# Value groups of the past, one at a time or in pairs, beside a dense prompt attention on one core

## The chip, the cores and the metric

The kernel runs on one core of one Trainium2 chip. The metric is device microseconds for one call, from the first to the last instruction on the core with what the runtime puts around it; lower is better. The engines are named as in the profile: PE (matmul), PEld (its weight loads), DVE (vector), ACT (scalar), POOL (GpSimd) and SP, which here computes nothing and only issues DMAs. Each engine executes its own instructions in the order in which they were written into its queue; what one engine needs from another is guarded by a semaphore.

## The reference, cut to what matters

One decoder layer is computed for 512 prompt tokens and for 8 sample tokens (one new token for each of 8 samples). Beside the prompt's own attention, each sample attends to 1024 past tokens that lie in 8 pages of 128 rows in a paged cache:

```python
v_all = jnp.concatenate([cache_v[page_table].reshape(DB, P, N_HEADS, HEAD_DIM), v], axis=1)
s = jnp.einsum("bqhd,bkhd->bhqk", q, k_all) * scale
s = s + Fk[:, :, P:, None] - Fk[:, :, None, :]
p = jax.nn.softmax(s, axis=-1)
return jnp.einsum("bhqk,bkhd->bqhd", p, v_all)
```

The last line, restricted to the past, is the part at issue: for 8 samples and 8 pages, a weighted sum over the 128 rows of a page of 1024 floats (512 KB), for each of 16 heads. Everything is float32; the dense products are made of three products of rounded halves (`hi`, `lo`) each.

## The kernel before, in words

Feature-major activations of 520 columns (512 prompt, 8 sample) stand in SBUF as 8 tiles of 128 partitions. The kernel runs one long list of products: `product()` takes one block of 128 weight columns, runs 24 matmuls over the first 260 columns, evacuates, and 24 over the second 260. `begin()`, at the head of each product, advances `state["n"]`, loads the weights ahead (`load_chunks`, on SP's queue) and splits them into halves ahead (`split_upto`: ACT writes `whi`, DVE writes `wlo`).

**The past's values.** The 8 samples go in four pairs `r`; pair `r` and page `j` make one *value group*, 32 groups in all (`values_todo`). `sample_values(r, j)` (L830 to L852) computes one group: four matmuls of 512 columns, each into its own 32 partitions of one PSUM bank `pv` through `tile_position=(0, 32 * gq)`, so that they use four strips of 32 columns of the array. A float32 matmul is two instructions in the trace, so that a group is eight PE instructions at L839. With the last page of a pair (`j == 7`) DVE masks and folds the bank into `dr`; two groups into the next pair (`j == 2`) `fold_values` runs one small matmul `pvs` (L854) and an ACT copy. `pw[r]`, the weights, comes from `past_softmax(r)`, a chain of steps of which `tick()` runs one at a time; `lgt` (L795) is one of its matmuls.

**The pages.** `page_load` reads a page's number into a register and issues one DMA of 512 KB into a tile of the pool `pgp` (7 buffers of 4 KB per partition, shared with pages of keys and, at other times, with other loads). Up to `state["n"] == 41` POOL issues it, later SP. `value_pages` loads one group ahead: its list `ahead` holds at most one group. The pool `heap` has 60 buffers ("slots") of 2080 bytes per partition, which `slot()` hands out for nearly all other tiles; an instruction that writes a tile waits until the last reader of the buffer's previous tile is through.

**When.** `tick(keys, values)` adds `values` to `state["due"]` and lets at most one group run. In the first 42 products it is called from `begin()`; ten groups run there. The attention then runs eight iterations `i`, one for each pair of heads. In iteration `i` the order on PE is: first half of the product `k` of `i+1`; **part 0** (`mid_a`: the transposes `vt` of `v_tokens`, then `at(i, 0)`); second half of `k`; the transposes `ptt` of `turn(i, 0)`; **part 1** (`at(i, 1)`); first half of the product `v`; `mid_b` with the transposes of `turn(i, 1)`, the scores of blocks 0 and 1 of `i+1` (L1245, L1246) and **part 2**; second half of `v`; `values(i)` (`po`, L1302); scores of blocks 2 and 3; **part 3** (`at(i, 3)`, not in the last iteration). In the last iteration the products are `gb`, and `turn(7, 0)` stands in part 0. The table `VALUES_AT` says how many groups fall due in each part: the remaining 22 groups run one by one in part 0 (8), part 1 (8) and part 3 (6). `in_place()` ties what a tick issues on PE, DVE and ACT behind the last product's matmul and the last split.

The steps that the prediction follows are the softmax of a pair of heads (DVE L1252, ACT L1253, reciprocal L1255, scaling by ACT or POOL at L1259), the casts of transposed probabilities (`ph` on ACT L1272, `pl` on DVE L1273) and the weight split (ACT L246, DVE L248).

Of the kernel before, what the change touches and what calls it, by code (L numbers as in the profile page):

```python
# [25 lines left out]
NPAGE = 8  # L26
# [39 lines left out]
def kernel(ctx, tc, xT, par, gates, b_f, cst, cse, own, cache_k, cache_v, cache_lf, pt,  # L66
# [13 lines left out]
    def slot(name, cols=NT, dt=F32, parts=128):  # L80
        return heap.tile([parts, cols], dt, name=name, tag="slot")

    def bank(name, parts=128, cols=512):
        return psp.tile([parts, cols], F32, name=name, tag="bank")
# [96 lines left out]
    state = {"n": 0, "dma": 0, "split": 0, "load": 22, "lead": 11, "due": 0, "age": 1}  # L181
# [8 lines left out]
    def flush():  # L190
        while stores:
            sp.dma_start(*stores.pop(0))
# [92 lines left out]
    def begin(last=None):  # L285
        n = state["n"]
        state["n"] += 1
        last = len(units) - 1 if last is None else last
        if n == 1:
            split_upto(reach(n, last, state["lead"]))  # L290
        if n < 42:
            tick(KEYS[n], n in VALUES)
        load_chunks(units[reach(n, last, state["load"])][0])
        split_upto(reach(n, last, state["lead"]))
        flush()
        return n
# [19 lines left out]
    @contextmanager  # L316
    def in_place():

        with tc.issue_after(state["mm"].ins), tc.issue_after(state["last"].ins), tc.issue_after(state["act"].ins):
            yield  # L320
# [371 lines left out]
    def page_load(cache, s, j, pg=None, c0=0, c1=D):  # L692
        if pg is None:
            pg = pgp.tile([128, D], F32, name="pg", tag="pg")
        n = s * NPAGE + j
        eng = pool if state["n"] <= LAST_POOL else sp
        done = loads[eng]
        with tc.issue_after(done[-4].ins) if len(done) >= 4 else nullcontext():
            r = eng.value_load(ptb[0:1, n:n + 1], min_val=0, max_val=NPOOL - 1)
        done.append(eng.dma_start(pg, cache[bass.ds(r, 1), :, c0:c1].rearrange("a p c -> (a p) c")))  # L700
        return pg
# [30 lines left out]
    def key_sums():  # L732
        for p in pend:
            p[0] += 1
        while pend and pend[0][0] >= (state["age"] if state["n"] < 43 else 1000):
            with tc.issue_after(state["qadd"].ins):
                key_sum()
# [19 lines left out]
    def key_pages(n):  # L757
        for _ in range(n):
            if keys_todo:
                key_page(*keys_todo.pop(0))  # L760
# [3 lines left out]
    chains = []  # L764
    pw = [None] * 4

    def tick(keys, values):
        state["age"] = 1 if state["n"] < 5 else 2
        key_sums()
        with in_place():  # L770
            for c in list(chains):
                c[0] += 1
                if c[0] >= 2:
                    c[0] = 0
                    if next(c[1], True):
                        chains.remove(c)
            state["due"] += values
            state["due"] -= some_values(min(1, state["due"]))
        value_pages()
        key_pages(keys)  # L780

# [50 lines left out]
    def sample_values(r, j):  # L832
        if j == 0:
            pv[0] = bank(f"pv{r}")
        pgs = ahead.pop(0)
        for gq in range(4):
            c = 32 * j + 8 * gq
            hf = gq % 2
            pe.matmul(pv[0][32 * gq:32 * gq + 32, :], lhsT=pw[r][:, c:c + 32],  # L839
                      rhs=pgs[gq // 2][:, 512 * hf:512 * hf + 512], start=j == 0, stop=j == NPAGE - 1,  # L840
                      tile_position=(0, 32 * gq))
        if j == NPAGE - 1:
            pw[r] = None
            dr = slot("dr", 512)
            dve.tensor_tensor(dr, pv[0], pvm, ALU.mult)
            for n in (256, 128):
                dve.tensor_tensor(dr[:, :n], dr[:, :n], dr[:, n:2 * n], ALU.add)
            pv["todo"] = r, dr
        elif j == 2 and "todo" in pv:
            fold_values(*pv.pop("todo"))  # L850

    def fold_values(r, dr):  # L852
        ps = bank(f"pvs{r}")
        pe.matmul(ps[:, :16], lhsT=dr[:, :128], rhs=cs[:, C_SEL:C_SEL + 16], start=True, stop=True)  # L854
        act.copy(pvt.rearrange("p (h c s) -> p c s h", h=2, c=4)[:, :, 2 * r:2 * r + 2],
                 ps[:, :16].rearrange("p (c s h) -> p c s h", c=4, s=2))

    values_todo = [(r, j) for r in range(4) for j in range(NPAGE)]
    ahead = []

    def value_pages():
        if values_todo and not ahead and (pw[values_todo[0][0]] is not None or chains):
            r, j = values_todo[0]
            ahead.append([page_load(cache_v, 2 * r + a, j) for a in range(2)])

    def some_values(n):
        done = 0
        while done < n and values_todo and pw[values_todo[0][0]] is not None:
            value_pages()
            sample_values(*values_todo.pop(0))  # L870
            value_pages()
            done += 1
        return done


# [500 lines left out]
    scores(0, (2, 3))  # L1376
    g = None
    state.update(load=14, lead=8)
    VALUES_AT = [(1, 1, 0, 1)] * 4 + [(1, 1, 0, 0)] + [(1, 1, 0, 1)] * 2 + [(1, 1, 0, 0)]
    KEYS_AT = [(0, 0, 2, 0)] * 3 + [(0, 0, 0, 0)] * 5  # L1380

    def at(i, part):
        tick(KEYS_AT[i][part], VALUES_AT[i][part])
        flush()

    for i in range(KT):
# [40 lines left out]
        if not last:  # L1427
            scores(i + 1, (2, 3))
            at(i, 3)
        else:  # L1430
            some_values(32)
            assert not values_todo and not chains
            fold_values(*pv.pop("todo"))
# [360 lines left out]
```

## Time and profile before

| | before |
|---|---|
| three timed runs | 1016.21, 1017.39 and 1019.45 us |
| median | 1017.39 us |
| span of the profiled execution | 1016.4 us, first to last instruction (its own time with what lies around the span is not listed apart from the three runs) |
| PE busy | 994.3 us, 98% of the span |
| DVE, ACT, POOL busy | 797.3, 547.5 and 327.6 us |
| attention, first to last value group in it | 355.23 us to 527.9 us of the span |

The page's shares of busy time are averages over the whole span; a PE row of the timeline shows start, duration, line, tile, shape and, in brackets, idle time before it and what ended that. The durations of matmul rows overlap, since matmuls are pipelined, so that the distance between two *starts* is what an instruction costs.

### The profile page before, as it was taken

The page shows a single profiled execution, that of the slowest core. Times are in us where ns is not written, and L with a number is a line of the kernel's source. Part 1 is how long each engine was busy: PE and PEld are TensorE (multiplying, and loading weights), DVE is VectorE, ACT ScalarE, POOL GpSimd, SP SyncE. Part 2 cuts the span into 40 slices and gives each one's busy share as a digit, 9 for nine tenths or more (in the row PEclk, how much of TensorE's full clock was granted, in tenths as well). Part 3 has the DMA queues.
Part 4 walks back from the last instruction along what each step waited for, and adds up shares of the span by engine and source line. Part 5 has one row for each costly group of instructions (what it writes and reads, how often), then busy time and mean ns, then how long its engine had stood idle before and what let it go on. Part 6 is the DMA issues. An engine that isn't in the chain of part 4 may idle for free.

```text
span 1016.4 us, 21281 instructions
## 1 busy us (share of the span) xinstructions
PE 994.3 (98%) x8012; PEld 921.1 (91%) x8012; DVE 797.3 (78%) x1423; ACT 547.5 (54%) x1128; POOL 327.6 (32%) x415
## 2 busy tenths in 40 slices
PE   5999999999999999999999999999999999999996
PEld 2799999999998988888888888999999999999996
DVE  5559999998999888886655544869988888888764
ACT  4534576848761576777783233554444444445553
POOL 0346111121143245653400001583442442425112
PEclk9999999999999999999999999999999999999998
DMA  9798857788879998995867995324234243233122
GB/s 325 250 324 279 242 189 202 243 261 278 281 250 345 331 312 286 321 294 190 251 216 269 319 340 186 84 74 115 81 108 125 63 125 98 70 104 105 63 64 85
DMA packets 164378, 206.97 MB, mean 204 GB/s; under 512 B 9827, under 2 KB 125043, under 8 KB 164211
## 3 DMA queue, kind: packets, MB, share of 16 engines
q1 hardware_dynamic: 147634, 152.78, 48.1%
q0 software_dynamic: 12960, 46.41, 13.8%
q10 hardware_dynamic: 3680, 6.42, 1.7%
q8 instruction: 63, 1.03, 0.4%
q14 instruction: 41, 0.33, 0.1%
HBM read 192.49 MB, written 13.09 MB: 202 GB/s over the span
## 4 chain that ended last, share of the span: by engine, by line
PE 93%; DMA 2%; DVE 2%; ACT 1%; issue 0%; SPq 0%; POOL 0%; DVEq 0%; POOLq 0%; ACTq 0%
PE fo L307 12%; PE k L307 5%; PE wo L307 5%; PE gb L307 5%; PE gr L307 5%; PE v L307 5%; PE ga L307 5%; PE xr L307 5%; PE pb L307 4%; PE pv L839 3%; PE pa L307 3%; PE po L1302 2%; PE qp L542 2%; PE q L542 2%; PE ada L374 2%; PE ptt L1268 2%
## 5 line engine op out<-in xcount | busy, mean ns | idle before, releaser
L246 ACT CAST whi<-wraw 128x1024 fp32r<-128x1024 f32 (+1 forms) x79 | 82.0, 1039 | 113.6 <-PE pb L307 34.3
L248 DVE TENSOR_TENSOR wlo<-wraw,whi 128x1024 fp32r<-128x1024 f32 (+1 forms) x79 | 99.1, 1256 | 19.0 <-ACT whi L246 16.6
L307 PE MATMUL fo<-ach,wb 128*128 128x260 f32 x512 | 93.4, 283 | 0.0
L270 ACT CAST wb<-ws 128x512 fp32r<-128x512 f32 x72 | 44.7, 621 | 86.0 <-PE fo L307 58.9
L700 POOL DMA_DIRECT2D pg<-in_cache_k_dram x74 | 39.6, 536 | 143.1 <-DVE S L751 62.6
L271 DVE TENSOR_TENSOR wb<-wraw,wb 128x512 fp32r<-128x512 f32 x86 | 76.4, 889 | 4.7 <-ACT wb L270 3.9
L307 PEld LDWEIGHTS fo<-ach,wb 128*128 128x128 f32 x512 | 78.9, 188 | 0.0
L271 DVE TENSOR_TENSOR wb<-ws,wb 128x512 fp32r<-128x512 f32 x72 | 68.7, 954 | 12.6 <-ACT wb L270 11.0
L261 POOL TENSOR_TENSOR ws<-wraw 128x512 f32<-128x512 f32 x18 | 24.4, 1353 | 153.2 <-DMA wraw<-in_w_fi_dram 104.1
L307 PE MATMUL fo<-acl,wb 128*128 128x260 f32 x256 | 72.2, 282 | 0.0
L270 ACT CAST wb<-wraw 128x512 fp32r<-128x512 f32 x86 | 53.5, 622 | 31.4 <-ACT cp L1683 6.2
L750 DVE TENSOR_TENSOR pg<-pg,qb 128x1024 f32<-128x1024 f32 x48 | 57.9, 1221 | 2.5 <-DMA pg<-in_cache_k_dram 2.5
L751 DVE TENSOR_REDUCE S<-pg 128x16 f32<-128x1024 f32 x48 | 57.4, 1209 | 0.2
L1259 POOL TENSOR_SCALAR p<-p,mu 128x128 f32<-128x128 f32 (+3 forms) x28 | 38.4, 1381 | 53.0 <-DVE mu L1255 47.1
L307 PEld LDWEIGHTS fo<-acl,wb 128*128 128x128 f32 x256 | 48.2, 188 | 0.0
L1253 ACT ACTIVATE p<-p,mu 128x128 f32<-128x128 f32 (+3 forms) x64 | 35.4, 554 | 18.2 <-DVE mu L1252 18.0
L307 PE MATMUL v<-hh,whi 128*128 128x260 f32 x128 | 38.2, 298 | 0.8 <-ACT row L819 0.5
L307 PE MATMUL k<-hh,whi 128*128 128x260 f32 x128 | 37.3, 292 | 0.0
L307 PE MATMUL pb<-oh,whi 128*128 128x260 f32 x128 | 37.1, 290 | 0.2 <-ACT oh L1360 0.2
L307 PE MATMUL gb<-hh,whi 128*128 128x260 f32 x128 | 37.0, 289 | 0.0
L307 PE MATMUL v<-hl,whi 128*128 128x260 f32 x128 | 36.9, 288 | 0.0
L307 PE MATMUL v<-hh,wlo 128*128 128x260 f32 x128 | 36.9, 288 | 0.0
(1101 smaller groups left out, 3957.3 us busy)
## 6 DMA issues: line engine op xcount, KB each, us to landing
araw<-in_ada_w_dram SPq DMA_DIRECT2D x48, 512.0 KB, 7.6
wraw<-in_w_fi_dram SPq DMA_DIRECT2D x44, 512.0 KB, 5.3
pg<-in_cache_k_dram POOLq DMA_DIRECT2D x42, 512.0 KB, 6.2
pg<-in_cache_v_dram SPq DMA_DIRECT2D x42, 512.0 KB, 5.5
wraw<-in_w_in_dram SPq DMA_DIRECT2D x34, 512.0 KB, 6.4
wraw<-in_w_in_dram SPq DMA_DIRECT2D x11, 1024.0 KB, 8.5
pg<-in_cache_v_dram POOLq DMA_DIRECT2D x22, 512.0 KB, 6.1
pg<-in_cache_k_dram POOLq DMA_DIRECT2D x32, 256.0 KB, 5.9
```

Of the source, the lines that this page charges most:

```text
L246: state["act"] = act.copy(hi[:, :k1 - k0], src)
L248: state["last"] = dve.tensor_tensor(lo[:, :k1 - k0], src, hi[:, :k1 - k0].bitcast(F32), ALU.subtract)
L270: state["act"] = act.copy(t[:, :4], src)
L271: state["last"] = dve.tensor_tensor(t[:, 4:], src, t[:, :4].bitcast(F32), ALU.subtract)
L307: state["mm"] = pe.matmul(out[:, :t1 - t0], lhsT=wt[k], rhs=at, start=k == 0 and m == 0, stop=k == nk - 1 and m == 2)
L542: state["mm"] = pe.matmul(b[:, :HALF], lhsT=wt, rhs=at[:, t0:t1], start=k == 0 and m == 0, stop=k == 3 and m == 2)
L700: done.append(eng.dma_start(pg, cache[bass.ds(r, 1), :, c0:c1].rearrange("a p c -> (a p) c")))
L750: dve.tensor_tensor(pg, pg, q, ALU.mult)
L751: last = dve.tensor_reduce(S[r // 2][:, c:c + H], pg.rearrange("p (h d) -> p h d", d=DH), AX.X, ALU.add)
L839: pe.matmul(pv[0][32 * gq:32 * gq + 32, :], lhsT=pw[r][:, c:c + 32], rhs=pgs[gq // 2][:, 512 * hf:512 * hf + 512], start=j == 0, stop=j == ...
L1253: act.activation(p[:, :n + 128], p[:, :n + 128], AF.Exp, bias=mu[:, 0:1], scale=-1.0, accum_out=mu[:, 1:2])
L1259: (pool.tensor_scalar(p, p, mu[:, 2:3], None, ALU.mult) if a and i + 1 < KT else act.activation(p, p, AF.Copy, scale=mu[:, 2:3]))
```

## The change

The ticks of the attention run two value groups back to back where they ran one: `depth()` is 2 from the 43rd product on, `tick` lets up to `depth()` groups run, and `VALUES_AT` makes the groups due in twos, in part 1 of every iteration and in part 3 of iterations 0, 2 and 4. Two groups are then loaded ahead. The first group's pages still go to `pgp`; each page of the second group is loaded in two halves of 512 columns into two slots of `heap`, by two DMAs of 256 KB. The matmuls themselves, their operands' shapes and their number stay.

```diff
             state["due"] += values
-            state["due"] -= some_values(min(1, state["due"]))
+            state["due"] -= some_values(min(depth(), state["due"]))
...
-                      rhs=pgs[gq // 2][:, 512 * hf:512 * hf + 512], start=j == 0, stop=j == NPAGE - 1,
+                      rhs=pgs[gq // 2][hf], start=j == 0, stop=j == NPAGE - 1,
...
+    def depth():
+        return 2 if state["n"] >= 43 else 1
+
+    def value_page(s, j, halves):
+        if halves:
+            return [page_load(cache_v, s, j, slot("pgv", 512), 512 * a, 512 * a + 512) for a in range(2)]
+        pg = page_load(cache_v, s, j)
+        return pg[:, :512], pg[:, 512:]
+
     def value_pages():
-        if values_todo and not ahead and (pw[values_todo[0][0]] is not None or chains):
-            r, j = values_todo[0]
-            ahead.append([page_load(cache_v, 2 * r + a, j) for a in range(2)])
+        while values_todo[len(ahead):] and len(ahead) < depth():
+            r, j = values_todo[len(ahead)]
+            if pw[r] is None and not chains:
+                break
+            ahead.append([value_page(2 * r + a, j, len(ahead) == 1) for a in range(2)])
 
     def some_values(n):
         done = 0
+        value_pages()
         while done < n and values_todo and pw[values_todo[0][0]] is not None:
-            value_pages()
+            if not ahead:
+                value_pages()
             sample_values(*values_todo.pop(0))
-            value_pages()
             done += 1
+        value_pages()
         return done
...
-    VALUES_AT = [(1, 1, 0, 1)] * 4 + [(1, 1, 0, 0)] + [(1, 1, 0, 1)] * 2 + [(1, 1, 0, 0)]
+    VALUES_AT = [(0, 2, 0, 2), (0, 2, 0, 0), (0, 2, 0, 2), (0, 2, 0, 0), (0, 2, 0, 2)] + [(0, 2, 0, 0)] * 3
```

## The prediction, made before the changed kernel was run

> **What bounds the kernel now.** I read the page first: the busy shares, then the chain of work that ended last.
>
> ```profile
> span 1016.4 us, 21281 instructions
> PE 994.3 (98%) x8012; PEld 921.1 (91%) x8012; DVE 797.3 (78%) x1423; ACT 547.5 (54%) x1128; POOL 327.6 (32%) x415
> PE 93%; DMA 2%; DVE 2%; ACT 1%; issue 0%; SPq 0%; POOL 0%; DVEq 0%; POOLq 0%; ACTq 0%
> ```
>
> PE works through 98% of the span and carries 93% of the chain. What the change takes from PE's queue is time, and what it makes PE wait for is time; nothing else counts directly. Next the tile `pv`:
>
> ```profile
> L839 PE MATMUL pv<-pg,pw x256: 589/593/617, 195.7 to 527.3; 128*32 128x512 f32 x128
> ```
>
> 256 instructions are 32 groups of eight; 22 of the groups lie in the attention. The 593 ns mislead, since four strips run beside each other. What a group costs is seen between the starts around it, in PE's timeline. Here are the end of the scores and the start of `k`, with a group between them and without one:
>
> ```profile
> 396.95 0.39 PE L1246 MATMUL sc<-ksB,qlB 128*128 128x512 f32 x1
> 397.27 1.06 PE L839 MATMUL pv<-pg,pw 128*32 128x512 f32 x8
> 398.27 0.39 PE L307 MATMUL k<-hh,whi 128*128 128x260 f32 x1
> 398.50 0.28 PE L307 MATMUL k<-hh,wlo 128*128 128x260 f32 x1
> ...
> 469.84 0.39 PE L1246 MATMUL sc<-ksB,qlB 128*128 128x512 f32 x1
> 470.07 0.28 PE L307 MATMUL k<-hh,whi 128*128 128x260 f32 x1
> 470.19 0.28 PE L307 MATMUL k<-hh,wlo 128*128 128x260 f32 x1
> ```
>
> From the last score to the second matmul of `k` it is 1.55 us with a group and 0.35 us without: **one group costs 1.20 us**. It starts late (0.32 us after a score, where `k` follows after 0.23), and the first `k` matmul behind it takes 0.23 us instead of 0.12.
>
> **The change part by part.** *Pairing.* No `pv` group follows another directly here, but the `ada` matmuls of the next stage have the same form (128x32 weights, 512 columns, four strips), and they run once as sixteen and then as eights:
>
> ```profile
> 543.21 0.28 PE L307 MATMUL pb<-ol,whi 128*128 128x260 f32 x1
> 543.42 1.92 PE L374 MATMUL ada<-araw,silc 128*32 128x512 f32 x16
> ...
> 545.50 0.28 PE L307 MATMUL pb<-oh,wlo 128*128 128x260 f32 x1
> ...
> 550.99 0.28 PE L307 MATMUL pb<-ol,whi 128*128 128x260 f32 x1
> 551.20 1.06 PE L374 MATMUL ada<-araw,silc 128*32 128x512 f32 x8
> ...
> 552.42 0.28 PE L307 MATMUL pb<-oh,wlo 128*128 128x260 f32 x1
> ```
>
> From the matmul ahead to the second one behind, eight take 552.42 - 550.99 = 1.43 us, less the two steps of 0.12 that would stand there anyway: 1.19. Sixteen take 545.50 - 543.21 = 2.29, less 0.24: 2.05. Two bursts apart cost 2.40, together 2.05, so **a clean pair saves 0.35 us** (the second eight cost 0.86).
> The Trainium skill, "TensorEngine Tiling (Array Packing)", section Key Properties, says that changing the tiling mode drains the array, which agrees with the rows. "TensorE: Matmul & The Clock Gate", Step-by-step, puts a drain at about 128 cycles; at its 2.4 GHz I estimate 0.05 us, so that eight spared bursts with two drains each would give 0.9 us. The measured rows decide for 0.35 each.
>
> *How many clean pairs.* The table asks for pairs in part 1 eight times and in part 3 three times. Groups 8 to 15 are `r` = 1, and so on; ten are done before, so the pairs are (10, 11), (12, 13), ... (30, 31). `fold_values` runs behind the group with `j == 2`, that is behind 10, 18 and 26: three pairs have the fold inside.
>
> ```profile
> 419.80 0.39 PE L1246 MATMUL sc<-ksB,qlB 128*128 128x512 f32 x1
> 420.12 1.06 PE L839 MATMUL pv<-pg,pw 128*32 128x512 f32 x8
> 421.12 0.39 PE L854 MATMUL pvs<-cs,dr 128*128 128x16 f32 x2
> 421.36 0.37 PE L307 MATMUL k<-hh,whi 128*128 128x260 f32 x1
> 421.57 0.28 PE L307 MATMUL k<-hh,wlo 128*128 128x260 f32 x1
> ```
>
> Group and fold cost 1.77 - 0.35 = 1.42, of which the fold is 0.22. The fold uses the whole array, so the mode changes twice inside the pair. With 0.09 lead, 1.00 group, 0.33 fold and second lead, 1.00 group and 0.11 slow restart I get 2.53 against 1.42 + 1.20 = 2.62: 0.1 saved, between 0 and 0.35. Eight clean pairs give 2.8 us, three split ones 0.3. The third pair of part 3, in iteration 4, meets `pw[3]` not yet set (its chain begins in part 2 of iteration 3 and sets it in part 0 of iteration 5); `due` keeps the two, and the pair runs in part 0 of iteration 5, still as a pair. In part 0 of iteration 4 `lgt`, a 128x32 matmul, loses the group beside it and pays its own change of mode: 0.2 us, between 0 and 0.35. PE's own work thus falls by 2.8 + 0.3 - 0.2 = **2.9 us**.
>
> *What the groups covered.* While PE ran a group, ACT and DVE prepared what PE needs next. From one `turn(i, 0)` to the next stood three groups (parts 1, 3, 0: 3.6 us); with a pair in part 1 alone stand 2.05, so that 1.55 us of cover go, in iterations 1, 3, 5 and 6 (0 and 2 keep part 3, and 4 has the delayed pair behind it). The slack is the end of the ACT scaling against PE's transposes:
>
> ```profile
> 449.82 1.22 ACT L1259 ACTIVATE p<-p,mu 128x384 f32<-128x384 f32 x2
> 452.03 1.03 PE L1268 MATMUL ptt<-cs,p 128*128 128x128 f32 x8
> ...
> 521.74 2.34 ACT L1259 ACTIVATE p<-p,mu 128x384 f32<-128x384 f32 x4
> 525.45 1.47 PE L1268 MATMUL ptt<-cs,p 128*128 128x128 f32 x12
> ```
>
> After iteration 3 the slack is 452.03 - 451.04 = 0.99, after iteration 6 it is 525.45 - 524.08 = 1.37. Less 1.55 each, PE waits 0.55 and 0.2 us, if ACT and DVE keep their distance from the end of `k`, to which the weight split ties them. I take **0.75 us lost**; 0 if they follow PE, 3.1 (twice the whole 1.55) if the tails of 1 and 5 are as tight.
>
> *What the pair covers in part 1.* In iteration 4 DVE masks the finished bank (`dr`) between two casts `pl`, and PE stands:
>
> ```profile
> 457.00 1.47 PE L1268 MATMUL ptt<-cs,p 128*128 128x128 f32 x12
> 459.39 0.39 PE L1245 MATMUL sc<-ksA,qqA 128*128 128x256 f32 x1 [0.16 <-DVE pl L1273]
> 460.42 0.69 PE L806 MATMUL lgm<-dg,cs 32*128 32x256 f32 x2
> 461.38 0.53 PE L307 MATMUL v<-hh,whi 128*128 128x260 f32 x1 [0.26 <-DVE pl L1273]
> 464.52 0.42 PE L307 MATMUL v<-hl,whi 128*128 128x260 f32 x1
> 464.74 0.35 PE L307 MATMUL v<-hh,whi 128*128 128x260 f32 x1
> ...
> 459.26 0.68 DVE L845 TENSOR_TENSOR dr<-pv,pvm 128x512 f32<-128x512 f32 x1
> ...
> 482.43 1.47 PE L1268 MATMUL ptt<-cs,p 128*128 128x128 f32 x12
> 484.66 0.30 PE L817 MATMUL lgs<-mk,cs 128*128 128x32 f32 x2
> ```
>
> The twelve transposes and eight scores take 3.42 us against 2.23 in iteration 5, and 0.26 idle follow: 1.45 us of stall. From 461.38 to 464.74 matmuls then stand 0.22 apart instead of 0.12, a clock near half; those 16 steps cost about 1.45 more. A pair in part 1 puts 0.85 us more before this place: **0.85 us gained**, 0 if DVE runs late by other causes, 2.9 if stall and slow clock both go. In iteration 1 the same `dr` (its first step takes 0.68) now falls into part 1 too, but under the longer pair and without a chain step beside it; I cost it at nothing and put 1.5 us into the range.
> On the clock the Trainium skill, "TensorE: Matmul & The Clock Gate", HAM oscillation, warns of idle gaps above some 3.4 us; the rows show a slow window after stalls of 1.45 us in all. By the page small new stalls would cost no clock, by the rows they can.
>
> *Pages.* Each second group is four DMAs of 256 KB instead of two of 512 KB: 22 more DMAs and 22 more reads of a page number, all on SP; POOL and ACT issue none of them. They are emitted after both groups, ahead of the `q` reloads and the next weights. At 0.34 us per issue these are 7.5 us of SP in 170, hidden, since SP mostly waits. The same bytes move.
>
> ```profile
> L700 SPq DMA_DIRECT2D pg<-in_cache_v_dram x42: 332/342/366, 348.1 to 503.2; - x42
> ...
> pg<-in_cache_k_dram POOLq DMA_DIRECT2D x42, 512.0 KB, 6.2
> pg<-in_cache_k_dram POOLq DMA_DIRECT2D x32, 256.0 KB, 5.9
> SPq L700 <- PE pv L839: 29.1, 14, 7.5
> ACT whi L246 <- DMA pg<-in_cache_v_dram: 2.8, 1, 2.8
> ```
>
> A half page takes about as long to land as a page, and the ticks with pairs lie half an iteration or more apart. SP stood 29.1 us until `pv` freed a buffer of `pgp`; half the pages leaving that pool eases this. Against it, a slot must be free: by my count of tile lifetimes in the program the 60 slots hold 33 to 42 tiles around the groups but 55 to 58 between parts 1 and 3 of iterations 2 to 5, where the next pair's four halves now lie as well. Then some `ph`, `p` or half page waits for a slot's last reader, and weights queue behind on SP. No row shows that wait; it lies between 0 and, by the one time ACT stood for weights behind pages, 2.8 us. I take **0.5 us**, nearer zero, since by the same row ACT stood so only once in the whole attention.
>
> *Sum.* -2.9 + 0.75 - 0.85 + 0.5 = **-2.5 us** on the profiled span of 1016.4. The median of the runs, 1017.39, is 1.0 above that span; I subtract from the median: **1014.9 us**.
>
> **The rivals.** *A, clean.* The stall and the slow clock of iteration 4 both vanish (-2.9), the tails hold (0), slots cost nothing: -2.9 - 2.9 = -5.8, 1011.6 us. For it: the slow stretch hangs on one window that a stall barely tips. Against it: 0.6 us of stall would remain by the sum.
> *B, cover lost; slower.* With parts 0 and 3 empty, PE reaches `turn` before the softmax after iterations 1, 3 and 6, and each stall tips the clock as in iteration 4. Price: three times 0.55 to 1.3 stall plus 1.45 clock, some 7.3 us, and -2.9 stays: about +4.4, 1021.8 us. It decides once a stall exceeds the 0.5 to 1.5 us that sufficed at 461.38. For it: a slack of 0.99 us against 1.55 lost. Against: the slack of the others is larger, and PE's transposes are the only consumers.
> *C, nothing.* Slots or weight loads eat the gain (2.5 us out of the 2.8 bound): 1017 us. That the change does not pair at all is possible only if the scheduler pulls other PE work between the two groups, as it does with `ptt` among `gb` in the last iteration; that too ends near 1017.
>
> **How the numbers follow.** A measurement tells about 0.3% (3.05 us) from no change; -2.5 lies just inside. Forecast (gains of 1 to 4 us) 0.47, A 0.23, C 0.16, B 0.14. A quarter of the forecast's case lies beyond 3.05 us: faster 0.23 + 0.12 = 0.35. Slower takes most of B: 0.13. Same: 0.52. The range reaches A's 1011.6 with a little above it left out below, 1011.5, and on the other side past C into the near part of B, 1019.5.
>
> **What would show it.** Right: eight rows `pv` x16 lasting about 1.92 us, three split by `pvs`; no `pv` in part 0 but at iteration 5; from the last score to the second matmul of `k` 0.35 us in iterations 1, 3, 6. Stalls on ACT L1259 before `ptt` in iterations 4 and 7 would show the lost cover, matmuls 0.22 apart behind them rival B, and rows of ACT or DVE released by late readers of slots, or `wraw` landing late, rival C. Wrong would be a second eight that costs over 1 us, or a slow clock elsewhere.

## The result, and the profile after

The changed kernel takes **1031.93 us** (median of four runs, 1030.44 to 1034.87) where the kernel before takes 1017.68 beside it (four runs, 1016.21 to 1019.45). The ratio is 1.0147, with a 95% interval of 1.0133 to 1.0162: 14 us slower. The forecast was 1014.9 us with a range to 1019.5, so both the sign and the range were wrong. The profiled execution took 1030.44 us. One run of an experiment below (half pages in `pgp`) took 1377.62 us at a granted clock of 0.657 and is left out of its median.

The page of the changed kernel, busy shares and the chain of work that ended last:

```profile
span 1028.8 us, 21436 instructions
PE 998.0 (97%) x8012; PEld 921.7 (90%) x8012; DVE 794.4 (77%) x1423; ACT 547.4 (53%) x1128; POOL 328.7 (32%) x415
PE 84%; DMA 6%; ACT 4%; DVE 3%; issue 2%; POOL 1%; POOLq 0%; SPq 0%; DVEq 0%; ACTq 0%
```

The span is 12.4 us longer, PE carries 84% of the chain instead of 93%, and DMA, ACT and DVE carry 13% where they had 5%: PE now waits for others. Its busy time is 3.7 us longer, and the rows at a slow clock and in pieces that are shown below are part of that; but the price of the pairs is the one that was forecast. Here is a clean pair (iteration 1) and one split by the fold (iteration 2), in PE's timeline:

```profile
392.91 1.06 PE L839 MATMUL pv<-pg,pw 128*32 128x512 f32 x8
393.80 1.04 PE L839 MATMUL pv<-pgv,pw 128*32 128x512 f32 x8
394.77 0.39 PE L307 MATMUL v<-hh,whi 128*128 128x260 f32 x1
...
430.08 1.07 PE L839 MATMUL pv<-pg,pw 128*32 128x512 f32 x8
431.08 0.39 PE L854 MATMUL pvs<-cs,dr 128*128 128x16 f32 x2
431.40 1.06 PE L839 MATMUL pv<-pgv,pw 128*32 128x512 f32 x8
432.40 0.39 PE L307 MATMUL k<-hh,whi 128*128 128x260 f32 x1
```

The clean pair lasts 394.77 - 392.91 = 1.86 us and the split one 432.40 - 430.08 = 2.32, which with the slower starts around them are the 2.05 and 2.53 of the prediction. What the change costs is found by stage. The table holds the time from the first `k` matmul of one iteration to that of the next (`gb` ends iteration 6, and iteration 7 goes from `gb` to the first `pb` matmul), worked out from the starts in PE's timeline; the four columns on the right belong to the experiments below.

| iteration | before | after | whole pages | cover kept | six groups left out | slots, cover kept |
|---|---|---|---|---|---|---|
| 0 | 23.61 | 34.02 | 24.39 | 23.41 | 23.48 | 24.91 |
| 1 | 22.85 | 21.39 | 23.52 | 22.46 | 22.33 | 28.89 |
| 2 | 23.09 | 25.37 | 24.74 | 22.75 | 23.60 | 23.41 |
| 3 | 23.06 | 21.39 | 21.79 | 22.51 | 21.95 | 24.19 |
| 4 | 25.65 | 23.71 | 23.48 | 22.70 | 23.66 | 23.93 |
| 5 | 23.65 | 26.80 | 24.47 | 23.41 | 23.61 | 26.31 |
| 6 | 22.78 | 21.32 | 22.62 | 22.53 | 23.18 | 26.21 |
| 7 | 20.44 | 23.04 | 23.07 | 21.16 | 22.14 | 23.91 |
| sum | 185.13 | 197.04 | 188.08 | 180.93 | 183.95 | 201.76 |

The attention accounts for 11.9 of the 12.4 us. A single group was put at 1.20 us, a pair at 2.05, a split pair at 2.53. By these, and by the number of groups that each iteration now holds, the eight iterations should change by +0.8, -1.55, +0.8, -1.55, -0.35, +0.8, -1.55 and -0.35, together -3.0. Iterations 1, 3 and 6 do just that (-1.46, -1.67, -1.46). Beyond these lie **iteration 0 with +9.6**, iteration 2 with +1.5, 5 with +2.4 and 7 with +2.9, and iteration 4, which gains 1.6. The two largest of PE's waits in this stage (line <- what it waited for: total, times, longest):

```profile
PE pv L839 <- DMA pgv<-in_cache_v_dram: 4.5, 1, 4.5
PE ptt L1281 <- ACT p L1272: 2.7, 4, 1.4
```

And PE's timeline in iteration 0:

```profile
363.02 1.48 PE L1281 MATMUL ptt<-cs,p 128*128 128x128 f32 x12
364.25 0.31 PE L1258 MATMUL sc<-ksA,qqA 128*128 128x128 f32 x1
...
369.15 2.58 PE L839 MATMUL pv<-pgv,pw 128*32 128x512 f32 x4 [4.48 <-DMA pgv<-in_cache_v_dram]
371.66 0.48 PE L1258 MATMUL sc<-ksB,qqB 128*128 128x128 f32 x1
371.93 0.42 PE L1259 MATMUL sc<-ksB,qlB 128*128 128x128 f32 x1
372.27 1.92 PE L839 MATMUL pv<-pgv,pw 128*32 128x512 f32 x2
374.12 0.48 PE L1258 MATMUL sc<-ksA,qqA 128*128 128x256 f32 x1
374.64 1.05 PE L839 MATMUL pv<-pgv,pw 128*32 128x512 f32 x2
```

Group 11, the second of the first pair, does not follow group 10. Its half pages come late, and its strips stand at three places among the scores of the next iteration, where PE runs them in order. The planner put them there: the scheduler that fixes the order of each engine's instructions when the kernel is built. PE pays three times. PE stands 4.48 us for the first half page. The group, which takes 1.0 us as eight rows, takes 2.58, 1.92 and 1.05 us in pieces of four, two and two: strips that aren't issued together don't run beside each other. And behind the gap the clock is near half (the profile has a granted clock of 0.50 from 369.2 to 372, and 1.00 from 376.5 on): the `sc` rows last 0.42 where they lasted 0.28, and two rows of `pv` last 1.92 where later two last 1.05. Instead of the 1.6 us that the kernel before spends from its first score to `v`, and 1.0 for the group, PE spends 12.3 (364.25 to 376.53, the first `v` row). Iteration 5 has the same picture without the gap and at the full clock: its pair falls due 5 us behind the delayed pair that ran in part 0, and group 27 runs in three pieces at 491.25, 493.04 and 494.66 among `ptt` and `sc`. Each piece takes 1.0 us, which makes some 2 of the 2.4 us.

Why the half pages are late stands in SP's own timeline, first of the kernel before and then of the changed one:

```profile
348.09 1.16 SPq L700 DMA_DIRECT2D pg<-in_cache_v_dram  x2
349.38 0.35 SPq L192 DMA_DIRECT2D tAd<-tA  x1
351.93 1.02 SPq L210 DMA_DIRECT2D wraw<-in_w_in_dram  x2
```

```profile
347.94 2.10 SPq L210 DMA_DIRECT2D wraw<-in_w_in_dram  x2
350.66 1.98 SPq L192 DMA_DIRECT2D tAd<-tA  x1
352.74 0.87 SPq L1228 DMA_DIRECT2D fb<-ftd  x2
360.94 1.01 SPq L210 DMA_DIRECT2D wraw<-in_w_in_dram  x2
362.22 3.30 SPq L700 DMA_DIRECT2D pgv<-in_cache_v_dram  x4
```

Before, the pages of the same group 11 (by count the first two of SP's 42 value pages) were issued at 348.09, ahead of a weight load. Now the halves stand behind two weight loads, and the second of them waits from 353.6 to 360.9 until DVE has split an earlier block and its buffer is free. In the changed kernel's list of SP's waits, within the attention alone, this is the largest by its total:

```profile
SPq L210 <- DVE wlo L248: 20.6, 4, 7.3
```

In the compiled program the halves' slots belonged last to the operands of branch A's final product, which PE has read before `k` starts at 351.62. At run time the slots were therefore free 10 us before SP came to the halves, and SP's timeline has no wait between the end of the weight load (361.95) and the first half (362.22): it was the place in SP's queue, and no longer the slot, that made them late. That place is the planner's choice.

### The profile page after: what moved, and what is told of

It reads as the page before. It is cut to its first block, busy times and chain, and to the rows that moved or that the text cites. A ratio compares the mean times of both kernels' runs of the same rounds, so it can differ in the third digit from the quotient of the medians.

```text
span 1028.8 us, 21436 instructions
## 1 busy us (share of the span) xinstructions
PE 998.0 (97%) x8012; PEld 921.7 (90%) x8012; DVE 794.4 (77%) x1423; ACT 547.4 (53%) x1128; POOL 328.7 (32%) x415
## 4 chain that ended last, share of the span: by engine, by line
PE 84%; DMA 6%; ACT 4%; DVE 3%; issue 2%; POOL 1%; POOLq 0%; SPq 0%; DVEq 0%; ACTq 0%
PE fo L307 12%; PE gr L307 5%; PE ga L307 5%; PE pb L307 4%; PE gb L307 4%; PE v L307 4%; PE wo L307 4%; PE k L307 3%; PE xr L307 3%; PE pv L839 3%; PE pa L307 3%; PE qp L542 2%; PE ada L374 1%; DMA pg<-in_cache_v_dram 1%; PE po L1315 1%
## 5 line engine op out<-in xcount | busy, mean ns | idle before, releaser
L248 DVE TENSOR_TENSOR wlo<-wraw,whi 128x1024 fp32r<-128x1024 f32 (+1 forms) x79 | 97.0, 1228 | 15.2 <-ACT whi L246 11.8
L271 DVE TENSOR_TENSOR wb<-ws,wb 128x512 fp32r<-128x512 f32 x72 | 62.1, 863 | 13.2 <-ACT wb L270 11.4
L1272 POOL TENSOR_SCALAR p<-p,mu 128x128 f32<-128x128 f32 (+3 forms) x28 | 36.3, 1308 | 56.1 <-DVE mu L1268 22.8
L1266 ACT ACTIVATE p<-p,mu 128x128 f32<-128x128 f32 (+3 forms) x64 | 35.3, 554 | 19.6 <-DVE mu L1265 19.5
L307 PE MATMUL xr<-hh,whi 128*128 128x260 f32 x128 | 36.8, 287 | 0.0
L307 PE MATMUL xr<-hh,wlo 128*128 128x260 f32 x128 | 36.3, 283 | 0.4 <-DVE wlo L248 0.4
```

The source lines that it names most:

```text
L248: state["last"] = dve.tensor_tensor(lo[:, :k1 - k0], src, hi[:, :k1 - k0].bitcast(F32), ALU.subtract)
L271: state["last"] = dve.tensor_tensor(t[:, 4:], src, t[:, :4].bitcast(F32), ALU.subtract)
L307: state["mm"] = pe.matmul(out[:, :t1 - t0], lhsT=wt[k], rhs=at, start=k == 0 and m == 0, stop=k == nk - 1 and m == 2)
L1266: act.activation(p[:, :n + 128], p[:, :n + 128], AF.Exp, bias=mu[:, 0:1], scale=-1.0, accum_out=mu[:, 1:2])
L1272: (pool.tensor_scalar(p, p, mu[:, 2:3], None, ALU.mult) if a and i + 1 < KT else act.activation(p, p, AF.Copy, scale=mu[:, 2:3]))
```

## The experiments

Two theories were tried, in four batches, each on another chip. **Slots**: half pages in slots of `heap` are issued late and hold up what shares a queue with them. **Cover**: groups moved away from parts 3 and 0 leave PE waiting for the softmax. Times of the kernel before beside each batch: 1016.51 us (first four runs), 1017.26 (next four), 1017.13 (next three), 1017.47 (last two).

### Whole pages for the second group

```diff
-            ahead.append([value_page(2 * r + a, j, len(ahead) == 1) for a in range(2)])
+            ahead.append([value_page(2 * r + a, j, False) for a in range(2)])
```

> The changed kernel with the second group's pages as full 512 KB pages in the pool pgp, no halves in slots; pairs and their places stay. Slot theory (the halves wait for slots that come free only when the last product of branch A has read its operands, their DMAs then stand behind a weight load on SP, and PE, in order, stands behind the late group): the waits on value pages at iterations 0 and 5 go, -10 to -14 us from the changed kernel, 1016 to 1021. Cover theory (the time went because parts 0 and 3 lost their groups): nothing comes back, about 1030.

Measured: 1021.70 us, ratio 1.0043 (1.0029 to 1.0057). Nine to ten of the fourteen us are gone with one word of the program (a little less than the 10 to 14 of the slot theory), iteration 0 is back at 24.39 (23.61 + 0.8), and iteration 5 at 24.47. The pairs, their places and the number of matmuls are the same. But 4 to 5 us over the kernel before remain, though PE has 3 us less to do. Beyond the price of the groups, iterations 1, 2, 6 and 7 lose 2.2, 0.9, 1.4 and 3.0 us. Iteration 1 still waits for pages, a little: its pair runs in pieces of eight, four and four rows and takes 3.95 us (384.33 to 388.28) where the pair of iteration 2 takes 1.85. In iterations 6 and 7 PE waits for ACT:

```profile
384.33 1.47 PE L839 MATMUL pv<-pg,pw 128*32 128x512 f32 x8
386.01 1.05 PE L839 MATMUL pv<-pg,pw 128*32 128x512 f32 x4 [0.21 <-DMA pg<-in_cache_v_dram]
387.30 1.05 PE L839 MATMUL pv<-pg,pw 128*32 128x512 f32 x4 [0.24 <-DMA pg<-in_cache_v_dram]
...
517.67 0.39 PE L307 MATMUL gb<-hh,whi 128*128 128x260 f32 x1 [1.11 <-ACT vt L335]
...
526.63 0.44 PE L1281 MATMUL ptt<-cs,p 128*128 128x128 f32 x2 [1.45 <-ACT p L1272]
```

### Earlier, later, or in a pool of their own

Three kernels keep the halves in slots or slot-like buffers and change when they are asked for. Single groups in iteration 0, two groups ahead only from product 44 on:

```diff
-        return 2 if state["n"] >= 43 else 1
+        return 2 if state["n"] >= 44 else 1
...
+    VALUES_AT = [(1, 1, 0, 0), (0, 2, 0, 2), (0, 2, 0, 2), (0, 2, 0, 0), (0, 2, 0, 0), (0, 2, 0, 2)] + [(0, 2, 0, 0)] * 2
```

> The changed kernel, halves in slots, but iteration 0 runs its two groups singly in parts 0 and 1 and the ten pairs begin in iteration 1 (part 1 of iterations 1 to 7, part 3 of 1, 2 and 5). Slot theory: every pair is asked for ten us or more ahead, after the heap has emptied, so both waits go: 1016 to 1020. Cover theory: the same or more stalls at the softmax tails, 1028 to 1031. Half-page theory (DMAs of 256 KB are what is slow): nothing comes back, 1030.

Two groups ahead one product earlier (42 instead of 43 in the same line):

> The changed kernel with depth() 2 from the 42nd product instead of the 43rd, so that the halves of group 11 are asked for one product sooner; all else stays, the split pair of iteration 5 too. Slot theory: only the 10.6 us of iteration 0 come back, about 1021. Half-page theory: 1030. Cover theory: 1030.

A pool of four buffers for the halves, with `heap` cut from 60 to 56 slots:

> The changed kernel with four buffers of their own for the halves, taken from the heap (56 slots left); half pages of 256 KB stay. Slot theory: group 11's halves are issued before the weight load, the 10.6 us of iteration 0 come back; with four buffers the pair of iteration 5, five us behind the pair before it, still waits: 1020 to 1023. Half-page theory: 1030. If 56 slots are too few for the rest of the kernel, over 1030.

Measured: 1023.99 us (ratio 1.0060 to 1.0094), 1026.75 (1.0082 to 1.0116) and 1027.79 (1.0079 to 1.0132). None of the three forecasts of the slot theory (1016 to 1020, about 1021, and 1020 to 1023 us) is met. In the first two PE no longer stands for a half page in iteration 0, which takes 22.50 us with its two single groups and 26.92 with two pairs (24.4 by their price). The first has whole pages there; in the second the halves of group 11 are issued at 345.67, ahead of the weight loads, so halves can come in time. But in all three something else is late later: iteration 5 takes 29.30, 26.78 (as in the changed kernel, 26.80) and 29.78 us. The wait in the first of them, and the clock behind it (`v` rows of 0.42 us that stand 0.22 apart, where 0.28 and 0.12 are usual):

```profile
486.16 0.41 PE L817 MATMUL lgs<-mk,cs 128*128 128x32 f32 x2 [3.13 <-DVE pl L1286]
486.84 0.59 PE L307 MATMUL v<-hh,whi 128*128 128x260 f32 x1 [0.26 <-ACT row L819]
487.22 0.42 PE L307 MATMUL v<-hh,wlo 128*128 128x260 f32 x1
```

The fourth kernel's attention starts 5.6 us late already (`k` at 357.37), with PE waiting for DVE ahead of it. Four slots fewer cost that much there, and the time of this run separates nothing. Its attention by itself takes 188.51 us where the changed kernel's takes 197.04: with buffers of their own the halves of group 11 are there, the group follows group 10 and the fold at once (365.84), and iteration 0 takes 25.19 us. The late start may have helped.

### Cover: pairs where they leave the softmax its burst

Whole pages as in the first experiment, and another table:

```diff
-    VALUES_AT = [(0, 2, 0, 2), (0, 2, 0, 0), (0, 2, 0, 2), (0, 2, 0, 0), (0, 2, 0, 2)] + [(0, 2, 0, 0)] * 3
+    VALUES_AT = [(0, 1, 0, 2)] * 4 + [(1, 1, 0, 0)] + [(2, 1, 0, 0)] * 2 + [(1, 1, 0, 0)]
```

> Six pairs instead of eleven, all pages whole in pgp, and the pairs placed so that every softmax tail keeps a burst ahead of its transposes: a pair in part 3 of iterations 0 to 3 (then part 0 is empty), single groups around iteration 4, a pair in part 0 of iterations 5 and 6, single groups in iteration 7; part 1 always keeps one group. Theory lost cover: 2.05 us of PE work stand ahead of each turn(i, 0) where before had 2.4 and the pairs of part 1 had 0 or 1.2, so no wait of ptt on ACT's scaling beyond 0.3 us, iterations 1 to 7 within 0.6 us of before each, and six times 0.35 us are gained: 1014.0 to 1016.0 us where the kernel before has 1016.5. Rival, pages: it is two groups' pages in flight at once that make loads and the engines behind them late, wherever the pair stands: 1019 to 1022, as with whole pages and pairs in part 1.

Measured: **1014.78 us**, ratio 0.9979 (0.9968 to 0.9989), faster than the kernel before, with six pairs where the slower kernel has eleven. Iterations 0 to 3, 5 and 6 gain 0.2 to 0.55 us each (table), as a pair should. Iteration 4 gains 2.95: the stall and the half clock that the prediction found there do not occur. That was not expected, and it is not the pairs' doing alone: in the profile of the variant below with five pairs that iteration takes 22.71 us too, while with single groups and the same early loads it keeps them. Which of its waits went first is not shown. Iteration 7 loses 0.7, half a microsecond of it on one wait:

```profile
518.51 0.44 PE L1281 MATMUL ptt<-cs,p 128*128 128x128 f32 x2 [0.50 <-ACT p L1272]
```

The end of the old table with the pairs of the changed one before it (one group in part 1 of iteration 5, parts 0, 1 and 3 of iteration 6, parts 0 and 1 of iteration 7):

> Whole pages in pgp and pairs in part 1 as in the first experiment, but the end of the table as in the kernel before: one group in part 1 of iteration 5 (behind the delayed pair in part 0), then parts 0, 1 and 3 of iteration 6 and parts 0 and 1 of iteration 7 with one group each. Theory lost cover: the 1.4 us of iteration 6 and 3.0 us of iteration 7 that the first experiment lost come back, less one pair's 0.35 or two: 1021.7 - 4.4 + 0.7 = 1018.0 (1017 to 1019), and no ptt waits on ACT in iteration 7; what iterations 1 and 2 lost (2.2 and 0.9) stays. Rival, a cause that isn't tied to these tails: 1020.5 to 1022.5.

Measured: 1018.33 us, ratio 1.0012 (1.0002 to 1.0022). The sum is as forecast, the parts only in half: iteration 7 takes 21.17 us where whole pages with pairs took 23.07, but iteration 6 takes 22.74 against 22.62, and iteration 1, whose code is the same, takes 21.91 against 23.52. The loss of iteration 1 in the first experiment's profile is thus no fixed price of the table; there the pages were late by a little, and here the pair takes 2.37 us instead of 3.95.

Then cover by itself: the kernel before, with the matmuls of six groups left out. Their values are missing from the output.

```diff
-        for gq in range(4):
+        for gq in range(0 if 8 * r + j in (12, 13, 21, 22, 29, 30) else 4):
```

> The kernel before without six of its groups' matmuls: groups 12, 13, 21, 22, 29 and 30 (parts 3 and 0 around the starts of iterations 1, 4 and 7) are loaded and not multiplied, so those values are missing from the output. No pair, no slot, no other page order. If PE's work were all, six times 1.20 us go: 1016.5 - 7.2 = 1009.3 us. Theory lost cover: with nothing ahead of turn(1, 0), turn(4, 0) and turn(7, 0) PE waits there for ACT's scaling (0.5 to 1.4 us each) and the clock falls behind one or two of them, so that 2 to 7 of the 7.2 us come back: 1011.5 to 1016.5 us, with waits of ptt on ACT in iterations 1, 4 or 7 that before does not have.

Measured: 1018.23 us, ratio 1.0006 (0.9993 to 1.0018). **Six groups, 7.2 us of PE work by the price of 1.20 each, were worth nothing.** That is beyond the upper end of what was expected. In the one profile the attention is 1.2 us shorter, not 7.2. It shows where the rest went, in iterations 6 and 7 above all, which lack groups 29 and 30 and take 0.4 and 1.7 us more. PE's waits of this kernel:

```profile
PE ptt L1268 <- ACT p L1259: 2.1, 2, 1.6
PE gb L307 <- ACT vt L335: 1.2, 1, 1.2
```

The same two rows, `ptt` on ACT's scaling and `gb` on `vt`, stood in the first experiment. They are waits that the groups of parts 3 and 0 had covered, and no pair and no slot is in this kernel to bring them about. (The pages of the six groups are still loaded; only, their buffers come free without PE.)

### Slots: the same, with the cover kept

Only the table of the kernel that ran at 1014.78 us, in the changed kernel:

> The changed kernel (second group's pages as halves in slots) with the table that keeps a burst ahead of every softmax tail: parts 1 and 3 of iterations 0 to 3 with one and two groups, one each in parts 0 and 1 of iteration 4, two and one in parts 0 and 1 of iterations 5 and 6, one each in iteration 7. Against the same table with whole pages (1014.8 us) only the place and the order of the page loads differ. Slot theory: group 11 is due in part 3 of iteration 0, near 373 us, and its halves land near 375 behind the weight load and the slots of branch A's operands, so it costs 1 to 3 us there instead of 10; later the slots and SP's order still delay loads at some places, 2 to 8 us in all: 1017 to 1024 us, with waits of pv on a half page or of k and v on weights. If half pages in slots cost nothing by themselves and only the missing cover did: 1014 to 1016 us.

Measured: 1034.25 us, ratio 1.0170 (1.0146 to 1.0194). Against whole pages with the same table the half pages in slots cost 19.5 us, far above the 2 to 8 that were expected. Iteration 0 behaves as forecast (24.91 against 23.41), and PE hardly waits for a page. The price is paid behind it, 6.4 us in iteration 1 (28.89 against 22.46) and 9.3 in iterations 5 to 7, which were not followed. ACT's timeline ahead of iteration 1, first with slots, then with whole pages:

```profile
365.71 0.17 ACT L819 COPY row<-lgs 1x32 f32<-1x32 f32 x1 [0.49 <-PE lgs L817]
372.22 0.54 ACTq L188 DMA_DIRECT2D mtd<-row  x1
372.86 0.40 ACT L1266 ACTIVATE p<-p,mu 128x128 f32<-128x128 f32 x1 [6.97 <-DMA pgv<-in_cache_v_dram]
```

```profile
365.83 0.17 ACT L819 COPY row<-lgs 1x32 f32<-1x32 f32 x1 [0.43 <-PE lgs L817]
366.04 0.51 ACTq L188 DMA_DIRECT2D mtd<-row  x1
366.76 0.40 ACT L1266 ACTIVATE p<-p,mu 128x128 f32<-128x128 f32 x1 [0.76 <-DVE mu L1265]
```

ACT has a small store of its own to issue, `mtd<-row`, which needs nothing but `row`. With slots it goes out 6.2 us later, and ACT's exponentials behind it wait 6.97 us, as the trace says, for a half page. In the compiled program the DMAs of SP and ACT count up eight semaphores in turn, and a DMA waits until the one that had its semaphore before has landed. The store's semaphore had gone to one of the halves that stood in SP's queue. So a late page stops ACT, and DVE stands behind ACT:

```profile
374.75 0.18 DVE L1268 RECIPROCAL mu<-mu 128x4 f32<-128x4 f32 x1 [7.25 <-ACT p L1266]
```

In iteration 1 PE then waits ahead of its transposes, 3.3 us in four waits, the longest of them for DVE. That these come from the stop of ACT and DVE is read from the order in time:

```profile
391.09 0.63 PE L1281 MATMUL ptt<-cs,p 128*128 128x128 f32 x4 [1.30 <-DVE ksB L1173]
```

PE did not stand for these pages themselves: the pair of iteration 0 starts at 373.20, and at 373.34 in the kernel with whole pages.

### Without pairs

The table and the single groups of the kernel before, pages loaded two groups ahead; first as halves in slots, then whole in `pgp`:

```diff
-            state["due"] -= some_values(min(depth(), state["due"]))
+            state["due"] -= some_values(min(1, state["due"]))
...
+    VALUES_AT = [(1, 1, 0, 1)] * 4 + [(1, 1, 0, 0)] + [(1, 1, 0, 1)] * 2 + [(1, 1, 0, 0)]
```

> No pairs: the table and the single groups of the kernel before, but from the attention on pages are loaded two groups ahead, the second as four halves in slots of the large pool. Slot theory: the first halves again wait in SP's queue behind the weight load and for slots that branch A's operands hold; group 11 is due in part 1, near 367 us, and its halves land near 374, so that PE waits 4 to 8 us there on the page, the rest as before: 1020 to 1026 us. Rival, pairing itself (both groups must be there at one moment): with single groups the early loading hides everything, no wait of pv on a page over 0.5 us, 1016 to 1018 us.

> No pairs: the table and single groups of the kernel before, whole pages in pgp, but loaded two groups ahead from the attention on. It separates the pairs' share from that of the earlier loads in the version that ran at 1014.8 us. If the pairs make the gain (six times 0.35 us = 2.1): 1016.3 to 1018 us, no difference from before beyond 0.1%. If the earlier loads or their place in SP's queue make it (by taking the stall and the slow clock of iteration 4 away): 1013.5 to 1015.5 us.

Measured: 1045.96 us with slots (ratio 1.0258 to 1.0300) and 1016.64 with whole pages (0.9988 to 1.0006). The former is far above its forecast of 1020 to 1026, and PE's waits for half pages are only 5.9 us of it. The two differ in the place of the pages (and the halving that goes with it) alone, by 29 us. All 84 loads of this stage are halves in the former. Against whole pages with the same table, 44 half loads cost 10 us (the changed kernel), 60 cost 19.5 (the experiment above) and 84 cost 29: the loss grows with the number of half loads. Pairing is not the harm. And loading earlier brings nothing by itself: with whole pages iteration 4 takes 25.34 us, with the stall and a granted clock of 0.57 behind it (0.51 in the kernel before). The 2.5 us of the kernel with six pairs come with the pairs and their places.

### Halves elsewhere

The changed kernel with its own table: the four DMAs of 256 KB kept, but into the two halves of whole buffers of `pgp`; and the halves in slots, but issued by POOL.

```diff
-            return [page_load(cache_v, s, j, slot("pgv", 512), 512 * a, 512 * a + 512) for a in range(2)]
+            pg = pgp.tile([128, D], F32, name="pg", tag="pg")
+            return [page_load(cache_v, s, j, pg[:, 512 * a:512 * a + 512], 512 * a, 512 * a + 512) for a in range(2)]
```

> The changed kernel with its own table (pairs in part 1), the second group's pages still loaded as four DMAs of 256 KB, but into two whole buffers of pgp instead of four slots. If the number and size of the DMAs cost the 10 us: 1029 to 1033 us, with pv waiting for a half page in iteration 0. If the slots (and the order on SP that follows from them) cost it: as with whole pages, 1020.5 to 1023 us, no wait of pv on a page over 0.5 us.

> The changed kernel with its own table and the halves in slots, but issued by POOL instead of SP, so that they stand behind no weight load and hold up nothing on SP. If SP's order is the cause: 1020 to 1025 us, group 11 of iteration 0 not waiting over 1 us. If the slots are held by others (in iteration 0 by branch A's operands, later by p and ph tiles): the halves of group 11 stay late and PE waits 2 us or more for a half page in iteration 0 or 5, 1027 to 1035 us.

Measured: 1022.50 us (ratio 1.0026 to 1.0055) and 1050.79 (1.0287 to 1.0345), the latter above both of its forecasts. Twice the DMAs at half the size cost nothing that these runs can tell (1021.70 with whole pages). Issuing by POOL makes it worse: PE waits 15.3 us for half pages, 6.4 at once in iteration 0, where POOL issues them at 364.85, behind its work on the decay rows:

```profile
364.29 0.46 POOL L1241 TENSOR_TENSOR fb<-fb,cs 128x128 f32<-128x128 f32 x1
364.85 3.81 POOL L700 DMA_DIRECT2D pgv<-in_cache_v_dram  x7
```

So taking the halves out of SP's queue does not bring them in time: with slots they stand late in POOL's queue too. The price of SP's queue alone can't be read from this run, since half pages that POOL issues also take longer to land (7.1 us against 5.5 in the changed kernel, by the medians of the pages).

### A better end of the table

Iteration 6 as in the kernel before, five pairs:

```diff
+    VALUES_AT = [(0, 1, 0, 2)] * 4 + [(1, 1, 0, 0), (2, 1, 0, 0), (1, 1, 0, 1), (1, 1, 0, 0)]
```

> As the version that ran at 1014.8 us, whole pages in pgp and cover kept, but iteration 6 with one group each in parts 0, 1 and 3, as in the kernel before, so that the last softmax tail has 2.4 us of groups ahead of it instead of 1.2: five pairs instead of six. By the lost cover: iteration 7 lost 0.7 us there (0.5 us wait of ptt on ACT), which comes back, less one pair's 0.35 us: 1014.0 to 1014.7 us, no wait of ptt on ACT in iteration 7. If that wait is not one of cover: 1015.1 us and the wait stays.

Measured: 1014.81 us, ratio 0.9981 (0.9970 to 0.9992). PE's wait on the scaling in iteration 7 is gone, but the time is that of six pairs, and iteration 7 takes 21.16 us as there: its first group now runs in pieces of two, three and three rows among the transposes (517.48 to 519.92). Between 1014.3 and 1015.1 the runs don't decide. Both tables with whole pages beat the kernel before by 0.2%, and the changed one by about 1.7%.

## Why the prediction was wrong, point by point

- **Pairing, -2.9 us: right.** Pairs cost what the `ada` rows said. Iterations 1, 3 and 6, in which nothing else changed, gained 1.46, 1.67 and 1.46 us where 1.55 was expected.
- **Pages, +0.5 us: the step that failed.** It said that the halves are emitted ahead of the `q` reloads and the next weights, and that their issue is hidden "since SP mostly waits". SP's waiting was the danger, not the cover: it waits in order, and what stands behind a waiting load waits with it. Nor is an issue only 0.34 us of SP: four halves, with the reads of their page numbers, take 3.30 (at 362.22). In the changed kernel the halves stand behind a weight load that waits 7.3 us for DVE, and they were due in the same part as the group ahead of them. The cost, forecast as 0.5 us, was 9.6 us in iteration 0 and 2.4 in iteration 5, and with slots against whole buffers 10.2 us in all (1031.93 against 1021.70, from two batches). The step also counted occupied slots, 33 to 42 at the groups and 55 to 58 later, and did not look at iteration 0, where the slots come from branch A's operands. And it took one wait of 2.8 us as the upper end, though that row comes from a queue with 42 value-page loads, where the changed kernel has 64.
- **Delayed pair: a gap in the same step.** That the pair due in iteration 4 runs in part 0 of iteration 5 was foreseen. That the next pair follows in part 1, 5 us later, and that its halves can't be there, was not. Iteration 5 ran 2.4 us over, most of it because group 27 ran in three pieces.
- **Lost cover, +0.75 us: right mechanism, too small.** In the changed kernel iterations 2 and 7 run 1.5 and 2.9 us over, and in both PE waits for the scaling ahead of `ptt` (1.1 and 1.4 us). The first is the tail of iteration 1, which the sum took as loose and the range alone as tight; and 4.4 us is beyond the 3.1 of its upper end. Iterations 1, 3 and 6 lose nothing there, each behind an iteration that ran over. With whole pages the attention takes 188.08 us in the table above, 2.95 more than before, though the groups should take 3.0 less and iteration 4 gains 1.8 beyond that (23.48 where 25.65 - 0.35 was due): some 7.8 us are lost elsewhere by that sum. Of these, 2.1 are the late pages of iteration 1; the other 5 to 6 lie mostly in iterations 2, 6 and 7, where PE's waits for ACT and DVE make some 3 of them. The slack of iteration 7 was read at the wrong row. The `ptt` x12 at 525.45 had 1.37 us, but two `ptt` ahead of them, which take the first scaled tile, had almost none. ACT ends that tile near 522.33 (521.74 and a quarter of 2.34), and PE's two transposes start at 522.40. ACT reaches it late because a table load and `sB` stand ahead of it. ACT's rows and PE's, of the kernel before:

```profile
520.16 1.28 ACT L1069 ACT_TABLE_LOAD   x1
521.45 0.39 ACT L1069 ACTIVATE sB<-gb 128x260 f32<-128x260 f32 x1
```

```profile
522.40 0.44 PE L1268 MATMUL ptt<-cs,p 128*128 128x128 f32 x2
```

  PE ran without a gap there because a group stood in front. The other tail that was read, of iteration 3, did better than forecast: ahead of the pair in iteration 4 of the changed kernel PE waits 0.28 us for it, where 0.55 was expected.
- **Relief in iteration 4, -0.85 us: right, too small.** The change gained 1.94 there in all, 1.6 beyond the smaller burst, and the granted clock is 1.00 through the iteration.
- **Rivals.** B gave the sign. That its 1021.8 us is the time with whole pages (1021.70) is luck: it rests on three stalls with a half clock behind each, and in that kernel's attention the granted clock is 1.00 and 2.1 us are late pages. C named slots and weights, with an upper end of 2.8 us where they cost 10. No case held both.

**What stays open.** Why the planner puts the halves so late when they go to slots, on SP and on POOL alike, was not found; that it does is read from the order alone. A kernel that keeps the slots and moves only the weight load behind the halves was not run. The nearest is the one that asks a product earlier, with iteration 0 at 26.92 us instead of 34.02. The part of SP's queue in the 10 us is so far argued from the traces, while the part of the slots is shown by runs. How the 5 to 6 us of lost cover divide between the iterations is open too, since one profile of each kernel differs by up to 1.6 us in an iteration with the same code.

## What to carry to other kernels

A load that moves to another pool moves in its queue as well: look at what stands ahead of it there, for how long that waits, and what comes behind, before its own cost is counted. When bursts are put together, price the places they leave by taking them out: work that an engine does while others prepare its next step can be free, as six groups here were. Read slack at the first row that uses the first tile, not at the longest row of the group.

## What had not been expected of the hardware and its program

- A group of eight rows takes 1.0 us in one go, and 1.05 us for two rows alone: the four strips run beside each other, and a group loses nearly all of that when the planner puts other work between them.
- An ACT store of one row was issued 6.2 us later because its semaphore had last gone to a half page that SP had not yet loaded. In this program queues that share no data are tied by that.
- The clock followed no single gap length. The granted clock was 0.50 for 4 to 5 us behind gaps of 4.48 us (changed kernel) and 3.13 us (single groups first), and in the kernel before 0.51 for 3.3 us behind 1.45 us of pieces. Behind waits of 1.11 and 1.45 us, 9 us apart (whole pages), it stayed 1.00. The Trainium skill, "TensorE: Matmul & The Clock Gate", section HAM oscillation, warns of gaps above some 3.4 us; the second of these gaps lies under that and the third far under it.
